# Mixture-of-experts stage: weight layout, the engines of the low parts and of the down loads, and the place of the gathers

## The chip, the core and the metric

The kernel runs on one core of one Trainium2 chip. The metric is device time in microseconds (us) of one execution. Engines are called TensorE (PE in the profile; PEld is its weight load), VectorE (DVE), ScalarE (ACT), GpSimd (POOL) and SyncE (SP, which only issues DMAs here).

## What is computed

The program is one encoder block over 1024 tokens of 1024 channels: a mixer (Hyena and SSD branches, projections, a gate), a layer norm, and a mixture of experts with a second layer norm. The change touches the experts. Cut to what matters, the reference has:

```python
idx, w = route(h2d, router_w, router_bias)      # 8 of 64 experts for each of 1024 tokens
def step(acc, blk):
    tok, wt, e = blk                             # up to 128 tokens of one expert
    xb = h_pad[tok]                              # gather
    hb = jax.nn.silu(xb @ w_gate[e]) * (xb @ w_up[e])   # 1024 -> 256, twice
    yb = (hb @ w_down[e]) * wt[:, None]          # 256 -> 1024
    return acc.at[tok].add(yb), None             # scatter-add
shared = (jax.nn.silu(h2d @ sh_w_gate) * (h2d @ sh_w_up)) @ sh_w_down
h = layer_norm(alpha * h + routed + shared)
```

All values are float32. Each expert has 3 MB of weights: gate and up of 1024 x 256 each, and down of 256 x 1024.

## The kernel before

The mixer and the router run first, and the experts last, in `moe`. Experts are taken by their rank in tokens; a table of capacities gives the 16 busiest 192 slots each, the next 160, 128 and 112. The order alternates a busy expert and a light one, so that a **round** of two experts has three **blocks**: 128 tokens, then 64 or 32 of the same expert, then 128 or 112 of the light one. There are 96 blocks in 32 rounds. The loop over b is written out by hand and sets each engine's order; nothing reorders it.

Float32 products are made of float32r parts: a value is split into a high part (ScalarE rounds it) and a low part (the rest, by a subtraction of two tiles), and a product takes three matmuls (`mm3`, lines 78 to 80), or two where 64 or 32 tokens leave room for both parts of the tokens side by side (`both_mm`, 1893 and 1895).

An expert's weights come in three **parts** p = 3i + q of 128 x 2048 values (1 MB): q = 0 and 1 hold gate and up of four k each, q = 2 holds down. For each part:

- `w_load` issues the load into `eraw` (three tiles for experts of either parity, so six parts are held). Parts 0 and 1 are issued by SyncE, as two DMAs of 512 KB whose pieces in the tile are 256 columns of gate and 256 of up in turn; part 2 by GpSimd, one DMA of 1 MB.
- `w_hi` (line 1643): ScalarE rounds `eraw` into `ehi`.
- `w_lo` (line 1650): `elo = eraw - ehi`, on VectorE for q = 0 and 1, on GpSimd for q = 2.

Step b of the loop handles parts 2b+2 and 2b+3. It issues in this order:

1. `gather(b + 3)`: GpSimd's indirect DMA of the tokens' rows into `xg` (line 1657). Block b's buffer is used again by block b+3.
2. `w_hi` of both parts.
3. The gate and up matmuls of block b, eight k of them. At k = 3 `lo_load(2b+2)`, that is `w_lo` and the load of the part six further, and then `hidden(b - 1)`: TensorE turns the hidden values of the block before, ScalarE and VectorE split them into `hb`.
4. The activation of block b: `swi_act`, or for a small block `both_act` with the tile `lows` (1906 to 1909).
5. `xpose(b + 2)`: eight transposes of the gathered tokens (line 1672), and their split.
6. `lo_load(2b + 3)`, one step of the slot tables of the next group of 12 blocks (one-hot comparisons of line 2103 on VectorE, small matmuls of 2111), if any is left.
7. `down(b - 1)`: the down matmuls of the block before, the copy into `yo` (two tiles), and the scatter-add into `scr_acc` on GpSimd (line 1693). The scatter-adds all write one tensor, and each waits until the one ahead has landed.

DMAs that GpSimd issues are in the profile's queue q0, those of SyncE in q1. On a queue of issues, a wait holds up everything behind it.

Of the kernel before, what the change touches and what calls it, by code (L numbers as in the profile page):

```python
# [9 lines left out]
F32 = mybir.dt.float32  # L10
# [31 lines left out]
class Kern:  # L42
# [1199 lines left out]
    def merge(self):  # L1242
# [106 lines left out]
        with ExitStack() as cx:  # L1349
# [136 lines left out]
                    sh[q] = [[v[:, h * 512:(h + 1) * 512] for v in hl] for h in range(2)]  # L1486

            def sh_gu(t):
                gu = [sh[k // 2][k % 2] for k in range(8)]
                for k, ps in enumerate(self.swi_gu(lhs(t), gu, P)):  # L1490
                    if k < 7:
                        yield
                yield self.swi_act(pool, ps, P, ld()[:, 0:256])
# [100 lines left out]
    def moe(self):  # L1594
# [3 lines left out]
        with ExitStack() as cx:  # L1598
# [17 lines left out]
            def w_load(p):  # L1616
                if p >= 192:
                    return
                i, q = divmod(p, 3)
                eng = nc.gpsimd if q == 2 else nc.sync  # L1620
                if q != 1:
                    weng[0] = eng.value_load(self.eid[0:1, order[i]:order[i] + 1], min_val=0, max_val=63)
                g, u, d = [a[n][0][bass.ds(weng[0], 1)].rearrange("o (p j) c -> (o p) j c", p=P)
                           for n in ("exp_w_gate", "exp_w_up", "exp_w_down")]
                parts = ((g[:, 0:4], u[:, 0:4]), (g[:, 4:8], u[:, 4:8]), (d,))[q]
                wraw[p] = rps[i % 2].tile([P, 2048], F32, name="eraw", bufs=3)
                v = wraw[p].rearrange("p (k c) -> p k c", k=parts[0].shape[1])
                c0 = 0
                for src in parts:
                    n = src.shape[2]  # L1630
                    eng.dma_start(v[:, :, c0:c0 + n], src)
                    c0 += n

            def w_hi(p, c=slice(0, 2048)):
                if p >= 192:
                    return
                if p not in whl:
                    i, q = divmod(p, 3)
                    hi, lo = whl[p] = [wps[i % 2].tile([P, 2048], F32R, name=f"e{c}", bufs=3) for c in ("hi", "lo")]
                    k = 2 if q == 2 else 4  # L1640
                    wsplit.setdefault(i, []).extend(zip(*[[v.rearrange("p (k c) -> p k c", k=k)[:, j] for j in range(k)]
                                                          for v in (hi, lo)]))
                nc.scalar.copy(whl[p][0][:, c], wraw[p][:, c])  # L1643

            def w_lo(p, c=slice(0, 2048)):
                if p >= 192:
                    return
                eng = nc.gpsimd if p % 3 == 2 else nc.vector
                hi, lo = whl[p]
                eng.tensor_tensor(lo[:, c], wraw[p][:, c], hi[:, c].bitcast(F32), ALU.subtract)  # L1650

            def gather(b):
                if b >= len(blocks):
# [28 lines left out]
            def down(b):  # L1682
# [1 line left out]
                    return  # L1684
                i, r, s, o, n = blocks[b]
                y = pool.tile([P, D], F32, name="yo", bufs=2)
                wd = [[(h[:, q * 512:(q + 1) * 512], l[:, q * 512:(q + 1) * 512]) for q in range(2)] for h, l in wsplit[i][8:10]]
                if n in (32, 64):
                    self.both_down(hbs.pop(b), wd, y, n)
                else:  # L1690
# [45 lines left out]
            for p in range(3, 6):  # L1736
                w_load(p)
            xpose(0)
            for p in range(2):
                for c in [slice(c * 512, c * 512 + 512) for c in range(4)]:  # L1740
                    w_hi(p, c)
                    w_lo(p, c)
                w_load(p + 6)
            xpose(1)
            tj = iter(())

            def lo_load(p):
                w_lo(p)
                w_load(p + 6)
            for b, (i, r, s, o, n) in enumerate(blocks):  # L1750
                if s == 0:
                    if i % 8 == 0 and i < 56:
                        for _ in tj:
                            pass
                        tj = table_jobs(i // 8 + 2)
                gather(b + 3)
                w_hi(2 * b + 2)
                w_hi(2 * b + 3)
                x, gu = xts.pop(b), wsplit[i][0:8]
                for k, ps in enumerate((self.both_gu if n in (32, 64) else self.swi_gu)(x, gu, n)):  # L1760
                    if k == 3:
                        lo_load(2 * b + 2)
                        hidden(b - 1)
                if n in (32, 64):
                    sgs[b] = self.both_act(pool, ps, tabs[r][s][2], n)
                else:
                    sgs[b] = self.swi_act(pool, ps, n)
                xpose(b + 2)
                lo_load(2 * b + 3)
                next(tj, None)  # L1770
                down(b - 1)
            for _ in tj:
                pass
# [80 lines left out]

    def swi_gu(self, lhs, gu, n):
        ps = self.bank()
        for k in range(8):
            self.mm3(ps[:n, :], lhs[k][0], lhs[k][1], gu[k][0], gu[k][1], k == 0, k == 7)
            yield ps

    def swi_act(self, pool, ps, n, sg=None):
# [34 lines left out]

    def both_gu(self, x, gu, n):
        ps = self.bank()
        for k in range(8):
            self.both_mm(ps, x[:, k], n, gu[k][0], gu[k][1], k == 0, k == 7)  # L1900
            yield ps

    def both_act(self, pool, ps, w, n):
# [499 lines left out]
```

## Time and profile before

| what | us |
|---|---|
| median of 3 runs (3575.53 to 3591.15) | 3579.17 |
| span of the profiled execution | 3579.6 |
| experts, in that span | about 2440 to 3520 |
| stretch read below as "the stage" | 2480 to 3520 |

The profile is of one execution. Busy time is the time in which an engine has an instruction of its own running; idle time before an instruction is put down to what released it. For TensorE the profile also gives the clock that was granted, as a share of full speed. For the DMA engines it gives packets, bytes, and the time that the packets took as a share of 16 engines.

### The profile page before, as it was taken

The page shows a single profiled execution, that of the slowest core. Times are in us where ns is not written, and L with a number is a line of the kernel's source. Part 1 is how long each engine was busy: PE and PEld are TensorE (multiplying, and loading weights), DVE is VectorE, ACT ScalarE, POOL GpSimd, SP SyncE. Part 2 cuts the span into 40 slices and gives each one's busy share as a digit, 9 for nine tenths or more (in the row PEclk, how much of TensorE's full clock was granted, in tenths as well). Part 3 has the DMA queues.
Part 4 walks back from the last instruction along what each step waited for, and adds up shares of the span by engine and source line. Part 5 has one row for each costly group of instructions (what it writes and reads, how often), then busy time and mean ns, then how long its engine had stood idle before and what let it go on. Part 6 is the DMA issues. An engine that isn't in the chain of part 4 may idle for free. (4 is left out here: it accounts for less than half of the span.)

```text
span 3579.6 us, 43779 instructions
## 1 busy us (share of the span) xinstructions
PE 3186.1 (89%) x15498; PEld 2534.1 (71%) x15499; DVE 2645.1 (74%) x3492; ACT 1462.2 (41%) x2335; POOL 1869.6 (52%) x1610
## 2 busy tenths in 40 slices
PE   8989989998998998998888999988898888898893
PEld 6767777777777776667778888876676666666662
DVE  6788887878787878557997254656787787786775
ACT  3333334343334232323334212324566655555663
POOL 2545454545454656445785140123676676776674
PEclk9999999999999999898889999988999999988996
DMA  4323243223232324734225345326999999988894
GB/s 130 77 71 91 65 90 89 75 76 88 75 84 67 94 77 123 218 124 170 72 71 165 124 165 160 102 72 217 269 264 273 272 262 265 261 246 247 252 283 125
DMA packets 440345, 541.44 MB, mean 151 GB/s; under 512 B 24409, under 2 KB 373373, under 8 KB 431165
## 3 DMA queue, kind: packets, MB, share of 16 engines
q1 hardware_dynamic: 404285, 376.08, 36.0%
q0 software_dynamic: 34688, 158.36, 15.3%
q10 hardware_dynamic: 1152, 4.19, 0.3%
q8 instruction: 123, 2.02, 0.2%
q14 instruction: 97, 0.79, 0.1%
HBM read 433.44 MB, written 105.12 MB: 150 GB/s over the span
## 5 line engine op out<-in xcount | busy, mean ns | idle before, releaser
L170 PE MATMUL bankA<-xth,whi 128*128 128x512 f32 (+1 forms) x1424 | 467.7, 410 | 0.4 <-DVE xtl L74 0.2
L170 PE MATMUL bankA<-xtl,whi 128*128 128x512 f32 (+1 forms) x1424 | 451.4, 399 | 0.0
L170 PE MATMUL bankA<-xth,wlo 128*128 128x512 f32 (+1 forms) x1424 | 447.3, 396 | 1.5 <-POOL wlo L74 1.5
L1650 DVE TENSOR_TENSOR elo<-eraw,ehi 128x2048 fp32r<-128x2048 f32 (+1 forms) x134 | 391.0, 2925 | 15.4 <-ACT ehi L1643 11.3
L1693 POOL DMA_INDIRECT scr_acc<-yo,sidx x96 | 231.3, 2410 | 284.7 <-DMA scr_acc<-yo,sidx 150.9
L74 POOL TENSOR_TENSOR wlo<-wraw,whi 128x1024 fp32r<-128x1024 f32 (+1 forms) x89 | 225.2, 2531 | 279.9 <-ACT whi L73 279.9
L1643 ACT CAST ehi<-eraw 128x2048 fp32r<-128x2048 f32 (+1 forms) x198 | 356.3, 1852 | 3.3 <-DVE sr L1505 3.3
L170 PEld LDWEIGHTS bankA<-xtl,whi 128*128 128x128 f32 (+1 forms) x1424 | 273.2, 192 | 63.7 <-DVE xtl L74 0.3
L170 PEld LDWEIGHTS bankA<-xth,wlo 128*128 128x128 f32 (+1 forms) x1424 | 271.3, 191 | 64.8 <-POOL wlo L74 1.9
L399 POOL TENSOR_SCALAR Wm<-cbm,dt 128x128 f32<-128x128 f32 x256 | 129.8, 507 | 347.2 <-DVE cbm L373 347.2
L170 PEld LDWEIGHTS bankA<-xth,whi 128*128 128x128 f32 (+1 forms) x1424 | 266.0, 194 | 58.0 <-issue 5.6
L1650 POOL TENSOR_TENSOR elo<-eraw,ehi 128x2048 fp32r<-128x2048 f32 x64 | 298.2, 4660 | 13.3 <-ACT ehi L1643 7.5
L78 PE MATMUL bankA<-ehi,xgh 128*128 128x512 f32 (+1 forms) x512 | 210.7, 412 | 0.0
L79 PE MATMUL bankA<-elo,xgh 128*128 128x512 f32 (+1 forms) x512 | 204.5, 399 | 6.0 <-DVE elo L1650 6.0
L80 PE MATMUL bankA<-ehi,xgl 128*128 128x512 f32 (+1 forms) x512 | 203.6, 398 | 0.0
L1657 POOL DMA_INDIRECT xg<-scr_h,gidx x96 | 166.7, 1737 | 63.3 <-issue 24.8
L1672 PE MATMUL bankB<-ident,xg 128*128 128x128 f32 (+3 forms) x768 | 113.8, 295 | 87.0 <-DMA xg<-scr_h,gidx 84.6
L1672 PEld LDWEIGHTS bankB<-ident,xg 128*128 128x128 f32 (+3 forms) x768 | 102.4, 198 | 115.3 <-issue 98.4
L74 DVE TENSOR_TENSOR xgl<-bankB,xgh 128x512 fp32r<-128x512 f32 (+1 forms) x128 | 81.2, 664 | 103.9 <-ACT xgh L73 95.7
L80 PE MATMUL bankA<-ehi,hb 128*128 128x512 f32 (+1 forms) x256 | 119.8, 468 | 28.9 <-DVE hb L74 28.9
L1909 DVE SCALAR_TENSOR_TENSOR lows<-lows,wt 64x256 f32<-64x256 f32 (+1 forms) x32 | 132.1, 4128 | 15.5 <-ACT lows L1908 15.5
L393 DVE SCALAR_TENSOR_TENSOR Em<-bcs,Acs,Em 128x128 f32<-128x128 f32 x256 | 141.1, 610 | 2.3
(586 smaller groups left out, 8410.5 us busy)
## 6 DMA issues: line engine op xcount, KB each, us to landing
eraw<-in_exp_w_gate_dram SPq DMA_DIRECT2D x128, 512.0 KB
eraw<-in_exp_w_down_dram POOLq DMA_DIRECT2D x64, 1024.0 KB, 5.3
eraw<-in_exp_w_up_dram SPq DMA_DIRECT2D x128, 512.0 KB
wraw<-in_w_in_dram SPq DMA_DIRECT2D x88, 512.0 KB
bcs<-scr_at SPq DMA_DIRECT2D x128, 256.0 KB
scr_K<-kout SPq DMA_DIRECT2D x32, 512.0 KB
Kt<-scr_K SPq DMA_DIRECT2D x32, 512.0 KB
scr_gate<-accf SPq DMA_DIRECT2D x16, 512.0 KB
```

Of the source, the lines that this page charges most:

```text
L74: (lo_eng or nc.vector).tensor_tensor(lo, src, hi.bitcast(F32), ALU.subtract)
L78: mm(out, sh, mh, start=first, stop=False)
L79: mm(out, sh, ml, start=False, stop=False)
L80: mm(out, sl, mh, start=False, stop=last)
L170: mm(ps[h], wt[:, k, :n], x[:, h * 512:(h + 1) * 512], start=(k == 0 and f == 1), stop=(k == KT - 1 and l == 1))
L393: STT(E[:, h], bcs[:, 1, h], self.A[:, c, 32 + j:33 + j], E[:, h], ALU.subtract, ALU.min)
L1643: nc.scalar.copy(whl[p][0][:, c], wraw[p][:, c])
L1650: eng.tensor_tensor(lo[:, c], wraw[p][:, c], hi[:, c].bitcast(F32), ALU.subtract)
L1657: nc.gpsimd.indirect_dma_start(out=t[:n, :], out_offset=None, in_=self.h_d, in_offset=bass.IndirectOffsetOnAxis(ap=tabs[r][s][0], axis=0))
L1672: nc.tensor.transpose(ps[:, j * P:j * P + n], free(t[:n, k:k + 1], [[8, P]]), self.ident[:n, :n])
L1693: nc.gpsimd.indirect_dma_start(out=self.acc_d, out_offset=bass.IndirectOffsetOnAxis(ap=tabs[r][s][1], axis=0), in_=y[:n, :], in_offset=Non ...
L1909: nc.vector.scalar_tensor_tensor(t[:, 0:256], t[:, 0:256], w, t[:, 256:512], ALU.mult, ALU.mult)
```

## The change

Five edits, all around the experts:

- **Layout of gate and up.** A part of gate and up lies in `eraw` as 1024 values of gate (four k) and then 1024 of up; each of its two DMAs has one 4 KB piece in every partition. The split tiles are read as two runs of 256 columns, one from each half, and the output bank is given in the same shape. The shared expert's tiles keep their place and are only given in that shape.
- **Low parts.** `w_lo` is on VectorE for all three parts.
- **Down weights.** All loads are issued by SyncE, in the order of the parts.
- **Gathers.** Step b issues `gather(b + 5)` right behind `xpose(b + 2)`, ahead of the scatter of block b-1. Blocks 3 and 4 are gathered before the loop. Since slot tables are needed sooner, the first two experts of a group make two table steps in each of their three steps.
- **Order at k = 3.** `hidden(b - 1)` is ahead of `lo_load(2b + 2)`.

```diff
             def sh_gu(t):
-                gu = [sh[k // 2][k % 2] for k in range(8)]
+                gu = [[v.rearrange("p (s c) -> p s c", s=2) for v in sh[k // 2][k % 2]] for k in range(8)]
...
-                eng = nc.gpsimd if q == 2 else nc.sync
-                if q != 1:
+                eng = nc.sync
+                if q == 0:
                     weng[0] = eng.value_load(self.eid[0:1, order[i]:order[i] + 1], min_val=0, max_val=63)
...
-                v = wraw[p].rearrange("p (k c) -> p k c", k=parts[0].shape[1])
-                c0 = 0
-                for src in parts:
-                    n = src.shape[2]
-                    eng.dma_start(v[:, :, c0:c0 + n], src)
-                    c0 += n
+                v = wraw[p].rearrange("p (s k c) -> p s k c", s=len(parts), k=parts[0].shape[1])
+                for n, src in enumerate(parts):
+                    eng.dma_start(v[:, n], src)
...
-                    k = 2 if q == 2 else 4
-                    wsplit.setdefault(i, []).extend(zip(*[[v.rearrange("p (k c) -> p k c", k=k)[:, j] for j in range(k)]
+                    k, n = (2, 1) if q == 2 else (4, 2)
+                    wsplit.setdefault(i, []).extend(zip(*[[v.rearrange("p (s k c) -> p k s c", s=n, k=k)[:, j] for j in range(k)]
                                                           for v in (hi, lo)]))
...
             def w_lo(p, c=slice(0, 2048)):
                 if p >= 192:
                     return
-                eng = nc.gpsimd if p % 3 == 2 else nc.vector
                 hi, lo = whl[p]
-                eng.tensor_tensor(lo[:, c], wraw[p][:, c], hi[:, c].bitcast(F32), ALU.subtract)
+                nc.vector.tensor_tensor(lo[:, c], wraw[p][:, c], hi[:, c].bitcast(F32), ALU.subtract)
...
             xpose(0)
+            gather(3)
...
             xpose(1)
+            gather(4)
...
-                gather(b + 3)
                 w_hi(2 * b + 2)
                 w_hi(2 * b + 3)
...
                     if k == 3:
+                        hidden(b - 1)
                         lo_load(2 * b + 2)
-                        hidden(b - 1)
...
                 xpose(b + 2)
+                gather(b + 5)
                 lo_load(2 * b + 3)
-                next(tj, None)
+                for _ in range(2 if i % 8 < 2 else 1):
+                    next(tj, None)
                 down(b - 1)
...
     def swi_gu(self, lhs, gu, n):
         ps = self.bank()
+        p3 = ps[:n, :].rearrange("p (s c) -> p s c", s=2)
         for k in range(8):
-            self.mm3(ps[:n, :], lhs[k][0], lhs[k][1], gu[k][0], gu[k][1], k == 0, k == 7)
+            self.mm3(p3, lhs[k][0], lhs[k][1], gu[k][0], gu[k][1], k == 0, k == 7)
...
     def both_gu(self, x, gu, n):
         ps = self.bank()
+        p3 = ps.rearrange("p (s c) -> p s c", s=2)
         for k in range(8):
-            self.both_mm(ps, x[:, k], n, gu[k][0], gu[k][1], k == 0, k == 7)
+            self.both_mm(p3, x[:, k], n, gu[k][0], gu[k][1], k == 0, k == 7)
```

How the instructions stand in the built programs, at three places in the middle of the experts. The first is GpSimd, a round before (`xg` is a gather, `scr_acc` a scatter-add, `elo` a low part, `eid` the expert's number that a load needs):

```order
L1693 DMA scr_acc<-yo,sidx_19823 1152x1024
L1657 DMA xg<-scr_h,gidx_20949 128x1024
L1650 TENSOR_TENSOR elo<-eraw,ehi 128x2048
L1622 TENSOR_LOAD eid
L1622 ISA x2
L1631 ISA
L1631 DMA eraw<-in_exp_w_down_dram 128x2048
L1693 DMA scr_acc<-yo,sidx_19810 1152x1024
L1657 DMA xg<-scr_h,gidx_20962 64x1024
```

and GpSimd now:

```order
L1653 DMA xg<-scr_h,gidx_20616 128x1024
L1689 DMA scr_acc<-yo,sidx_19801 1152x1024
L1653 DMA xg<-scr_h,gidx_20629 64x1024
L1689 DMA scr_acc<-yo,sidx_19814 1152x1024
L1653 DMA xg<-scr_h,gidx_20616 128x1024
```

Nothing is left on GpSimd between a gather and a scatter; what these rows don't tell is that the gather is now for the block six further than that of the scatter behind it, where it was for the one five further than that of the scatter ahead of it.

The second is VectorE over the steps of a small block's followers before (`hb` is the split of the hidden values, `xgl` and `xgh` that of the tokens, `sg` the activation, `yo` the output):

```order
L1650 TENSOR_TENSOR elo<-eraw,ehi 128x2048
L74 TENSOR_TENSOR hb<-bankC,hb 128x2x64
L1866 TENSOR_TENSOR sg<-sg,bankA 128x256
L74 TENSOR_TENSOR xgh<-bankB,xgh 128x4x64 x2
L1650 TENSOR_TENSOR elo<-eraw,ehi 128x2048
L1931 TENSOR_TENSOR yo<-yo,bankA 64x512 x2
L74 TENSOR_TENSOR hb<-bankC,hb 128x256
L1866 TENSOR_TENSOR sg<-sg,bankA 128x256
```

and VectorE now:

```order
L74 TENSOR_TENSOR hb<-bankC,hb 128x2x64
L1646 TENSOR_TENSOR elo<-eraw,ehi 128x2048
L1866 TENSOR_TENSOR sg<-sg,bankA 128x256
L74 TENSOR_TENSOR xgh<-bankB,xgh 128x4x64 x2
L1646 TENSOR_TENSOR elo<-eraw,ehi 128x2048
L1932 TENSOR_TENSOR yo<-yo,bankA 64x512 x2
L74 TENSOR_TENSOR hb<-bankC,hb 128x256
L1646 TENSOR_TENSOR elo<-eraw,ehi 128x2048
L1866 TENSOR_TENSOR sg<-sg,bankA 128x256
```

The subtraction stands behind `hb` and no longer ahead of it, and every step has two of them.

The third is SyncE, the loads of one expert before:

```order
L1622 TENSOR_LOAD eid
L1622 ISA x2
L1631 ISA
L1631 DMA eraw<-in_exp_w_gate_dram 128x4x256
L1631 ISA
L1631 DMA eraw<-in_exp_w_up_dram 128x4x256
```

and SyncE now:

```order
L1629 DMA eraw<-in_exp_w_gate_dram 128x1024
L1629 ISA
L1629 DMA eraw<-in_exp_w_up_dram 128x1024
L1629 ISA
L1629 DMA eraw<-in_exp_w_down_dram 128x2048
L1622 TENSOR_LOAD eid
L1622 ISA x2
```

A gate or up load has rows of 1024 values, and the down load stands behind both parts of gate and up.

## Rows read from the trace of the kernel before

**Rows 1.** Busy us of each engine (instructions), granted clock, DMA share, GB/s, by stretch.
```profile
2480.00:3520.00 1040.00, 919.81 (x4599) 691.16 (x4598) 798.75 (x788) 620.93 (x779) 713.22 (x308) 0.93 0.89 256
2600.00:2700.00 100.00, 89.64 (x463) 70.22 (x463) 79.17 (x78) 59.71 (x74) 70.71 (x31) 0.90 0.93 268
200.00:300.00 100.00, 94.59 (x429) 76.47 (x429) 76.63 (x123) 38.15 (x69) 46.94 (x60) 0.94 0.34 84
2000.00:2100.00 100.00, 100.00 (x437) 81.90 (x437) 39.03 (x40) 22.84 (x34) 37.73 (x40) 1.00 0.41 135
```
**Rows 2.** TensorE's waits from 2480 to 3520: us in total, times, longest.
```profile
PE bankB L1672 <- DMA xg<-scr_h,gidx: 84.6, 30, 5.4
PE bankA L80 <- DVE hb L74: 23.4, 18, 1.8
```
**Rows 3.** Groups from 2480 to 3520: busy us, mean ns, idle us before.
```profile
L1650 DVE TENSOR_TENSOR elo<-eraw,ehi 128x2048 fp32r<-128x2048 f32 x124 | 372.8, 3010 | 11.4 <-ACT ehi L1643 11.3
L1643 ACT CAST ehi<-eraw 128x2048 fp32r<-128x2048 f32 x186 | 344.6, 1904 | 0.0
L1650 POOL TENSOR_TENSOR elo<-eraw,ehi 128x2048 fp32r<-128x2048 f32 x62 | 287.8, 4642 | 1.1
L1909 DVE SCALAR_TENSOR_TENSOR lows<-lows,wt 32x256 f32<-32x256 f32 (+1 forms) x31 | 131.6, 4246 | 15.0 <-ACT lows L1908 15.0
L2103 DVE TENSOR_TENSOR oh<-iota,posm 128x1536 bf16<-128x1536 int16 (+1 forms) x54 | 79.7, 1477 | 0.0
```
**Rows 4.** GpSimd's timeline, 2800 to 2836: start, us, instruction, idle before.
```profile
2803.20 0.58 POOL L1631 DMA_DIRECT2D eraw<-in_exp_w_down_dram  x1 [0.30 <-POOL elo L1650]
2804.08 2.45 POOL L1693 DMA_INDIRECT scr_acc<-yo,sidx  x1 [0.30 <-issue]
...
2814.64 0.59 POOL L1631 DMA_DIRECT2D eraw<-in_exp_w_down_dram  x1 [0.30 <-POOL elo L1650]
2816.38 4.29 POOL L1693 DMA_INDIRECT scr_acc<-yo,sidx  x1 [1.15 <-ACT ehi L1643]
2820.97 1.00 POOL L1657 DMA_INDIRECT xg<-scr_h,gidx  x1 [0.30 <-issue]
2829.95 1.46 POOL L1693 DMA_INDIRECT scr_acc<-yo,sidx  x1 [7.99 <-DVE sg L1866]
```
**Rows 5.** Landing of the scatter issued at 2804.08, from its start.
```profile
DMA to landing us min/median/max: 11.5/11.5/11.5
```
**Rows 6.** Landing of the scatter issued at 2816.38, from its start.
```profile
DMA to landing us min/median/max: 12.8/12.8/12.8
```
**Rows 7.** Landing of the scatter issued at 2829.95, a small block's.
```profile
DMA to landing us min/median/max: 4.8/4.8/4.8
```
**Rows 8.** TensorE's timeline, 2800 to 2836.
```profile
2809.32 0.50 PE L80 MATMUL bankA<-ehi,hb 128*128 128x512 f32 x1 [1.17 <-DVE hb L74]
...
2831.02 1.13 PE L1672 MATMUL bankB<-ident,xg 128*128 128x128 f32 x8 [2.31 <-DMA xg<-scr_h,gidx]
```
**Rows 9.** TensorE's timeline, 2468 to 2480.
```profile
2475.90 0.80 PE L80 MATMUL bankA<-ehi,hb 128*128 128x512 f32 x1 [5.48 <-DVE hb L74]
```
**Rows 10.** VectorE's timeline, 2440 to 2480.
```profile
2468.92 6.60 DVE L1650 TENSOR_TENSOR elo<-eraw,ehi 128x2048 fp32r<-128x2048 f32 x1
...
2476.92 0.48 DVE L1909 SCALAR_TENSOR_TENSOR lows<-lows,wt 64x256 f32<-64x256 f32 x1 [0.48 <-ACT lows L1908]
```
**Rows 11.** VectorE's timeline, 2800 to 2836.
```profile
2816.89 2.27 DVE L1650 TENSOR_TENSOR elo<-eraw,ehi 128x2048 fp32r<-128x2048 f32 x1
```
**Rows 12.** DMA queues from 2480 to 3520: packets, MB, share of 16 engines.
```profile
q0 software_dynamic: 29934, 138.08, 46.1%
q1 hardware_dynamic: 127168, 126.90, 42.3%
```
**Rows 13.** The only data queue from 2817 to 2818 (1 KB pieces).
```profile
q1 hardware_dynamic: 380, 0.38, 108.3%
```
**Rows 14.** The only queue from 2840 to 2842 (8 KB pieces).
```profile
q0 software_dynamic: 96, 0.79, 100.7%
```

More of the change, by code (lines that the diff above doesn't have):

```diff
@@ L1686, in down @@
                 y = pool.tile([P, D], F32, name="yo", bufs=2)
-                wd = [[(h[:, q * 512:(q + 1) * 512], l[:, q * 512:(q + 1) * 512]) for q in range(2)] for h, l in wsplit[i][8:10]]
+                wd = [[(h[:, 0, q * 512:(q + 1) * 512], l[:, 0, q * 512:(q + 1) * 512]) for q in range(2)] for h, l in wsplit[i][8:10]]
                 if n in (32, 64):
```

## The prediction

> **What bounds the kernel now.** I began with the busy time of each engine by stretch, since the change touches the experts alone. In the 1040 us from 2480 to 3520, where the experts run, TensorE is busy 919.81 us, so it is idle for 120.2; VectorE is busy 798.75, GpSimd 713.22, and the 16 DMA engines 89% [rows 1]. No engine is full, so the question is who holds up whom. The waits of TensorE come next: 84.6 of the 120.2 idle us stand before the transposes of the gathered tokens, until a gather has landed, in 30 places; another 23.4 are for `hb`, the low part that VectorE makes of the hidden values [rows 2]. The rows of `lows<-lows` say how many rounds the stretch holds: 31 [rows 3]. A round is an expert of two blocks and an expert of one (three steps of the block loop), and takes 1040/31 = 33.5 us. So one of the three gathers in each round is late.
>
> Why it is late is read from GpSimd's timeline. The scatter-add of 2816.38 is issued 0.8 us after the one of 2804.08 has landed (it takes 11.5 us), the next, 2829.95, 0.8 us after the landing of the second (12.8 us) [rows 4 to 7]. Scatter-adds go into one tensor, each waits for the one ahead, and GpSimd works in order: the gather stands behind it and is issued only at 2820.97. TensorE reaches the transposes that need it and waits 2.31 us, until 2831.02 [rows 4, 8]. The weights are not late: ScalarE, which rounds them first, was idle 0.0 us before its casts [rows 3].
>
> Two more things are to be seen. Where VectorE and GpSimd both subtract, both suffer: the same 128x2048 subtraction takes 2.27 us on VectorE beside a scatter and 6.60 beside GpSimd's own subtraction [rows 10, 11]; the small product into `lows` takes 0.48 us once and 4246 ns in the mean [rows 3, 10]. And TensorE's granted clock is 0.93 in the stage, against 1.00 in a stretch where it is busy for 100 of 100 us and 0.94 where it is busy for 94.59 [rows 1]: with its idle time it loses 0.07 x 1040 = 73 us of full rate (a mean of its two levels, 2.4 GHz at 1.00 and 1.2 GHz).
>
> **The change, part by part.** All sums are against the profiled execution, whose span of 3579.6 us lies within 0.5 us of the median 3579.17.
>
> Gathers ahead. The gather of block b+5 is now issued in step b, ahead of the scatter of block b-1; before, it was the gather of b+3, behind the scatter of b-2. It gains two steps, some 22 us. It adds a wait: its buffer is that of block b+2, freed by transposes that TensorE has just been given. Behind that wait on GpSimd stands only the scatter of b-1, whose matmuls come after the same transposes, so nothing is held up that was free. I take off all 84.6 us. The table work runs ahead too: in three of a group's twelve steps it is issued twice. In such a round VectorE has six one-hot comparisons of 1477 ns, 8.9 us, beside 6 x 2.27 of subtractions and its other work: (798.75 - 372.8 - 131.6 - 79.7)/31 = 6.9 us a round, and 0.5 for `lows` [rows 1, 3, 10, 11]. That is 29.9 us, about the whole of the new round; I add 1.5 us in each of seven groups, +10 (0 to 25).
>
> Low parts on VectorE. GpSimd loses 287.8 us of subtractions, VectorE gains 62. If all 186 run at 2.27 us, they are 422 us in place of 372.8, and `lows` falls from 131.6 to 31 x 0.48 = 15. VectorE ends at 798.75 - 372.8 - 131.6 + 422 + 15 = 731 us: less than before, since the collision goes. At the old mean of 3010 ns it would be 560 + 294 + 132 = 986 of 1040; I take 731, because the slow ones in the rows stand beside GpSimd's subtraction and the quick one beside a scatter [rows 3, 10, 11].
>
> `hidden` ahead of the subtraction. The `hb` wait of 1.17 us at 2809.32 is shorter than the 2.27 us subtraction that stood ahead of it [rows 8, 11]. But the subtraction that GpSimd did is now ahead in the step before. Of 23.4 us [rows 2] I take off 18 (between all of it and +10). Ahead of 2480 one more such wait goes, 5.48 us behind a subtraction of 6.60: -5 [rows 9, 10].
>
> Down weights from SyncE. GpSimd no longer issues them (0.58 us each [rows 4]); SyncE issues them in the order of the parts, behind gate and up of the same expert, when the subtraction of the part six earlier is done; no load waits for a later part than before. They leave the queue that the scatters use. That cannot be priced from one row: the two scatters with a down load just ahead of them land 9.0 and 8.5 us after their issue is written, the one without 3.3, though it moves half the rows [rows 4 to 7]. I count nothing for it; it is what makes room in a rival below.
>
> Long runs. Gate and up now lie as 4 KB pieces. In the stage q1's 126.90 MB take 42.3% of 16 x 1040 us, 55 ns a KB (1000 bytes); in a stretch with nothing but 1 KB pieces it is 45.6 ns, in one with 8 KB pieces 40.8 [rows 12 to 14]. So the gain is 10% to 26% of 440 us of every DMA engine's time: 47 to 117. I take 53, near the low end, since the price of contention stays. On TensorE the moving operand of a gate and up matmul is now two runs of 256 columns; no row shows one. I take nothing; each 10 ns on 64 of them a round would cost 31 x 64 x 10 = 20 us. At the start the first chunk of a part no longer holds gate and up of one k: the first matmuls wait for two more quarter subtractions (0.57 us) in each of two parts, +3.
>
> Clock. With most of the idle time gone I expect some of the 73 us back, and take -25 (0 to -73): the stretch at 94.59% still has 0.94 [rows 1].
>
> **The sum.** TensorE's side of the stage: 1040 - 84.6 - 18 + 10 - 25 = 922 us. The DMA side: 0.89 x 1040 = 926, less 53 is 873 us of work; the highest share that a stretch of 100 us shows is 0.93 [rows 1], and at that it takes 938. The larger ends last: the stage falls by 102, the start gives -5 + 3. 3579.6 - 104 = 3475 us. What is late next is then the weights, held by the DMA engines, with TensorE close behind.
>
> **Rivals.** (a) More comes back: the clock in full and the low price of long runs. TensorE 1040 - 84.6 - 23.4 - 73 = 859, DMA (926 - 117)/0.93 = 870: 170 less, 3410. Against it: both extremes at once.
>
> (b) Long runs give nothing, and the DMA engines are the bound: 926/0.93 = 996, 44 less and 2 for the start, 3533. For it: with 0.93 they are near full already. Against it: the pure stretches differ.
>
> (c) The scatter chain stays as it is. It asks 11.5 + 12.8 + 4.8 + 3 x 0.8 = 31.5 us a round [rows 5 to 7], so 31 x 31.5 = 977: 63 less, 65 with the start, 3514. The gathers no longer wait, but the output buffers (two) do, and TensorE behind them. Then the move of the down loads has not shortened a landing. The Trainium skill (DMA: Bandwidth & Descriptors, "Issuing engines are not separate DMA queues") says that issuing from another engine saves only the issuing sequencer's time; by that, this case is the one to expect. The landings of 9.0 and 3.3 us after issue speak against the rule, though the rows moved differ.
>
> (d) Slower: the scatter chain grows. A scatter is written in 1.46 us when VectorE is at other work and in 4.29 beside a subtraction [rows 4, 11]. VectorE now subtracts for 422 us of some 930. If every scatter took 4.29 and landed as late as now, the chain would be 31.5 + 1.84 + 2.83 = 36.2 us a round, 1121 in all: 81 more, 3659. It decides from 33.5 us a round, so when the three grow by over 2 us together. Against it: the two slow landings should shorten without the down loads ahead. The Trainium skill (SBUF — State Buffer, "Who interferes with whom") holds that a subtraction of two SBUF inputs takes only the read side of the shared port, and that writing descriptors wants the other; by that this case could not be. Here the trace differs: 4.29 us beside one, 1.46 without.
>
> **How the numbers follow.** The forecast, 3475, has 0.58 and by itself runs from 3435 to 3510; (a) 0.12; (b) 0.10; (c) 0.13; (d) 0.05; small changes from other mishaps 0.02. The range of 8 in 10 leaves out (d), the lower half of (a) and the rest: 3425 to 3545. About 0.5%, 18 us, is what a measurement of this kernel can tell from no change. Below 3561 lie the forecast, (a), (b) and (c): faster 0.92; same 0.03; slower 0.05.
>
> **What would show it.** Right: TensorE's wait on gathers near nothing; the VectorE subtraction at a mean of about 2.3 us and `lows` under 0.6; q1 under 50 ns a KB; landings of large scatters well below 11 us; a clock above 0.95. Wrong: waits of ScalarE's casts on the weights (b), of the output copies or GpSimd on the scatter ahead all the time (c, d), or gate and up matmuls longer than 410 ns at full clock.

## The result, and the profile after

The changed kernel takes 3613.65 us (median of 5 runs, 3609.53 to 3617.34); the kernel before took 3579.17 (3568.96 to 3591.15) on the same chip. The ratio is 1.0092, with a 95% interval of 1.0069 to 1.0115: slower by 0.9%, more than the 0.5% that the prediction takes as tellable from no change, 139 us above the forecast and 69 above the upper end of the range. The profiled execution has a span of 3615.6 us.

The expert stage by stretch, for the whole stage and for one round and a half of it; columns as in [rows 1]:

```profile
2480.00:3520.00 1040.00, 884.61 (x4478) 676.30 (x4476) 707.31 (x833) 596.50 (x757) 332.82 (x180) 0.91 0.84 252
2732.00:2780.00 48.00, 32.81 (x171) 26.01 (x171) 30.18 (x30) 22.22 (x29) 13.97 (x8) 0.82 0.84 252
```

TensorE is idle for 155 us of the 1040, against 120 before [rows 1], and its mean clock fell from 0.93 to 0.91. GpSimd is busy for less than half of what it was, VectorE for 91 us less, and the other engines and the DMAs are less busy too, in part since the longer stage puts less of itself into the 1040 us (182 weight subtractions in all, where it was 124 + 62). In the 48 us from 2732 TensorE is busy for only 32.8. So something new is waited for. TensorE's waits from 2480 to 3520 (us in total, times, longest) are now these, in place of [rows 2]:

```profile
PE bankD L2112 <- DVE oh L2104: 128.8, 20, 9.2
PE bankA L78 <- ACT hb L73: 26.5, 9, 4.3
```

The 84.6 us for the gathers are gone, and so are the 23.4 for the low part of `hb`. In their place stand 128.8 us in 20 places, before the small matmuls of the routing tables (L2112), until VectorE has made a one-hot. In the kernel before that wait came to 7.1 us in 8 places, 1.5 at the longest:

```profile
PE bankD L2111 <- DVE oh L2103: 7.1, 8, 1.5
```

The groups of the stage (busy us, mean ns, idle us before), which answer [rows 3]:

```profile
L1646 DVE TENSOR_TENSOR elo<-eraw,ehi 128x2048 fp32r<-128x2048 f32 x182 | 415.1, 2281 | 0.3
...
L2104 DVE TENSOR_TENSOR oh<-iota,posm 128x1536 bf16<-128x1536 int16 (+1 forms) x54 | 78.5, 1484 | 0.0
...
L2112 PE MATMUL bankD<-aux,oh 128*128 128x6 bf16 (+1 forms) x656 | 32.5, 175 | 128.8 <-DVE oh L2104 128.8
...
L1910 DVE SCALAR_TENSOR_TENSOR lows<-lows,wt 64x256 f32<-64x256 f32 (+1 forms) x31 | 14.7, 475 | 15.0 <-ACT lows L1909 15.0
```

The one-hots are as many and as quick as before: 54 of 1.48 us. They are not made late because VectorE is full (707 of 1040 us). They are late because of where they stand.

### One pass of the loop, read from three timelines

The 48 us from 2732 show it. TensorE (start, us, instruction, idle before):

```profile
2755.41 0.90 PE L2112 MATMUL bankD<-aux,oh 128*128 128x6 bf16 x16 [6.03 <-DVE oh L2104]
...
2765.34 0.34 PE L2112 MATMUL bankD<-aux,oh 128*128 128x6 bf16 x8
2774.84 0.89 PE L2112 MATMUL bankD<-aux,oh 128*128 128x6 bf16 x16 [9.16 <-DVE oh L2104]
...
2776.68 0.63 PE L80 MATMUL bankA<-ehi,hb 128*128 128x512 f32 x1
...
2779.95 0.39 PE L79 MATMUL bankA<-elo,hb 128*128 128x512 f32 x1
```

ScalarE:

```profile
2759.25 0.69 ACT L1688 ACTIVATE yo<-bankA,wt 128x512 f32<-128x512 f32 x1 [9.19 <-PE bankA L80]
2760.72 0.69 ACT L1688 ACTIVATE yo<-bankA,wt 128x512 f32<-128x512 f32 x1 [0.78 <-PE bankA L80]
2761.30 3.69 ACT L1640 CAST ehi<-eraw 128x2048 fp32r<-128x2048 f32 x2
2764.90 0.38 ACT L73 ACTIVATE hb<-bankC 128x256 fp32r<-128x256 f32 x1
```

VectorE:

```profile
2765.31 0.42 DVE L74 TENSOR_TENSOR hb<-bankC,hb 128x256 fp32r<-128x256 f32 x1 [8.82 <-ACT hb L73]
2765.65 2.28 DVE L1646 TENSOR_TENSOR elo<-eraw,ehi 128x2048 fp32r<-128x2048 f32 x1
...
2769.62 1.29 DVE L74 TENSOR_TENSOR xgl<-bankB,xgh 128x512 fp32r<-128x512 f32 x2
2770.83 2.28 DVE L1646 TENSOR_TENSOR elo<-eraw,ehi 128x2048 fp32r<-128x2048 f32 x1
2773.03 2.89 DVE L2104 TENSOR_TENSOR oh<-iota,posm 128x1536 bf16<-128x1536 int16 x2
```

Read them in a circle. At 2755.41 TensorE gets its one-hot and does the table matmuls and the down matmuls behind them. At 2759.25 ScalarE, idle for 9.19 us, can copy the first half of their result; behind the copies stand the casts of two weight parts (3.69 us) and behind these the copy into `hb`, 2764.90. VectorE, idle for 8.82 us, takes `hb` and then, in its order, a weight subtraction, the small work of `lows`, `xgl`, a second subtraction and at 2773.03 the two one-hots. The first is ready when TensorE's table matmuls start, 2774.84; the down matmuls stand behind these, and the circle begins again. TensorE's share is 3.8 us (to 2759.25), ScalarE's 6.1 (to 2765.31), VectorE's 9.5 (to 2774.84): 19.4 us for a step of the block loop, where a step took 33.5/3 = 11.2 in the kernel before. Each of the three engines is idle for some 9 us or more of it. (The eight table matmuls of 2765.34 wait for nothing: they are those of the block's first table step, whose one-hot was made in the block before.)

Why the change closes this circle: a table step makes the one-hot of a slot r and issues the matmuls of slot r-1. With one table step to a block of the loop, the one-hot had been made a block earlier. With two in a block, the second step's matmuls need the one-hot that the first step of the same block makes, and that stands last in VectorE's block. Program order had given a lead of one block, and the change took it away in three blocks of every group of twelve. Behind such a wait the next down matmuls run 0.63 us each and then 0.39 again; the granted clock is 0.50 from 2775.60 to 2779.60 (the lower level, 1.2 GHz), after 9.16 idle us, and 0.99 from 2779.70 to 2784. So the lower level of the clock is paid too.

### The profile page after: what moved, and what is told of

The parts are those of the page before. It is cut to its first block, busy times and chain, and to the rows that moved or that the text cites. A ratio compares the mean times of both kernels' runs of the same rounds, so it can differ in the third digit from the quotient of the medians.

```text
span 3615.6 us, 43535 instructions
## 1 busy us (share of the span) xinstructions
PE 3179.0 (88%) x15499; PEld 2540.3 (70%) x15499; DVE 2564.1 (71%) x3556; ACT 1455.5 (40%) x2335; POOL 1487.9 (41%) x1482
## 3 DMA queue, kind: packets, MB, share of 16 engines
q10 hardware_dynamic: 1152, 4.19, 0.3%
## 5 line engine op out<-in xcount | busy, mean ns | idle before, releaser
L1689 POOL DMA_INDIRECT scr_acc<-yo,sidx x96 | 199.2, 2074 | 617.0 <-DMA scr_acc<-yo,sidx 161.2
L1646 DVE TENSOR_TENSOR elo<-eraw,ehi 128x2048 fp32r<-128x2048 f32 (+1 forms) x198 | 438.2, 2216 | 6.9 <-ACT ehi L1640 6.6
L74 DVE TENSOR_TENSOR hb<-bankC,hb 128x256 fp32r<-128x256 f32 (+3 forms) x96 | 34.8, 362 | 295.4 <-ACT hb L73 295.4
L1653 POOL DMA_INDIRECT xg<-scr_h,gidx x96 | 152.9, 1593 | 211.8 <-PE bankB L1668 78.4
L1688 ACT ACTIVATE yo<-bankA,wt 128x512 f32<-128x512 f32 (+1 forms) x128 | 84.5, 691 | 205.2 <-PE bankA L80 151.5
L2112 PE MATMUL bankD<-aux,oh 128*128 128x6 bf16 (+1 forms) x672 | 33.4, 175 | 134.3 <-DVE oh L2104 134.3
L430 DVE TENSOR_TENSOR yt<-yt,off 128x256 f32<-128x256 f32 x112 | 136.0, 1214 | 3.9
L394 ACT ACTIVATE Em<-Em 128x512 f32<-128x512 f32 x64 | 40.4, 631 | 224.8 <-DVE Em L393 224.8
```

Of the source, the lines that this page charges most:

```text
L74: (lo_eng or nc.vector).tensor_tensor(lo, src, hi.bitcast(F32), ALU.subtract)
L430: TT(y, y, off[:, d], ALU.add)
L1646: nc.vector.tensor_tensor(lo[:, c], wraw[p][:, c], hi[:, c].bitcast(F32), ALU.subtract)
L1653: nc.gpsimd.indirect_dma_start(out=t[:n, :], out_offset=None, in_=self.h_d, in_offset=bass.IndirectOffsetOnAxis(ap=tabs[r][s][0], axis=0))
L1689: nc.gpsimd.indirect_dma_start(out=self.acc_d, out_offset=bass.IndirectOffsetOnAxis(ap=tabs[r][s][1], axis=0), in_=y[:n, :], in_offset=Non ...
```

## The experiments

The theory: the lost lead of the table steps costs what the result shows, and without it the rest of the change gains. The rival: the new load and order of VectorE, the queues or the scatters are to blame, and the wait at L2112 only shows what is late anyway. All ratios are to the kernel before on the same chip.

### One table step a block (e1), and the doubled step alone (e2)

e1 is the changed kernel with one table step in each block; the tables of a group are begun two experts earlier so that they are ready in time.

```diff
-                    if i % 8 == 0 and i < 56:
+                    if (i == 0 or i % 8 == 6) and i < 54:
...
-                        tj = table_jobs(i // 8 + 2)
+                        tj = table_jobs((i + 2) // 8 + 2)
...
-                for _ in range(2 if i % 8 < 2 else 1):
+                for _ in range(2 if i < 2 else 1):
                     next(tj, None)
```

> The changed kernel, but with one table step in a block: a group's tables are begun three blocks earlier (at the seventh expert of the group before) in place of two steps in each of three blocks. Only the first group, which has no group before it, keeps the two steps. Theory A (lost lead): in the changed kernel the small table matmuls stand in the very step in which VectorE makes their one-hot, so TensorE waits for VectorE, VectorE for the hidden values, these for ScalarE and ScalarE for TensorE's down matmuls; with the lead of one step back, TensorE's wait of 128.8 us on one-hots goes, every round is about as long as the undisturbed ones (27 us, against 42 and 46 in each group's first two), and some 200 to 240 us go: 3375 to 3415. Theory B (VectorE has too much to do with six comparisons in a round): the same, since the comparisons are spread. Theory C (the loss is from something else, scatters or weights): 3550 or more, and the wait moves elsewhere.

Measured: 3479.62 us, 0.9719 (0.9703 to 0.9736). e2 is the kernel before with the doubled step and nothing else of the change:

```diff
-                next(tj, None)
+                for _ in range(2 if i % 8 < 2 else 1):
+                    next(tj, None)
```

> The kernel before with one edit: two table steps in each of the first three blocks of a group. Theory A: the same loop closes here too, at about 20 places; 6 us each and the clock behind them, less what the late gathers hid: 3640 to 3740. Theory B: VectorE has 25.8 us of work in a round of 33.5, and three comparisons more are 4.4 us, which fit: 3575 to 3600.

Measured: 3693.80 us, 1.0316 (1.0298 to 1.0333). TensorE's waits in e1, 2480 to 3380, and then in e2, 2480 to 3520:

```profile
PE bankA L78 <- ACT hb L73: 48.3, 22, 4.2
PE bankD L2112 <- DVE oh L2104: 4.9, 2, 4.7
```
```profile
PE bankD L2112 <- DVE oh L2104: 137.6, 20, 9.1
PE bankB L1672 <- DMA xg<-scr_h,gidx: 53.4, 25, 4.5
```

The same wait, again in 20 places, appears in the kernel before with that one line, and all but goes from the changed kernel without it (4.9 us in 2 places). The doubled step costs 115 us in the one (within what was expected) and 134 in the other. That settles the sign. e1 gained less than was expected of it (3375 to 3415): with the wait gone, something else held the stage.

### The same two steps, with the lead kept (e3)

e1 also spreads VectorE's one-hots. e3 keeps both table steps in the same blocks, with the same work, and only lets the matmuls follow two steps behind their one-hot and go ahead of the next one.

```diff
-        late = None
-        for r, caps in group + [(None, None)]:
-            if late:
+        wait, lag = [], 1 if ohs else 2
+        for step, (r, caps) in enumerate(group + [(None, None)] * lag):
+            if step:
                 yield
+            if step >= lag:
+                r0, caps0, oh0 = wait.pop(0)
+                ...
             if r is not None:
                 ...
                 TT(oh, ...)
-            if late is not None:
-                r0, caps0, oh0 = late
-                ...
-            late = (r, caps, oh)
+                wait.append((r, caps, oh))
```

> The changed kernel with its two table steps in a block, but the matmuls of an expert's table are issued two table steps behind its one-hot, so always in a later block. VectorE and TensorE have the same work in the same blocks. Theory A: the wait on one-hots goes, 3375 to 3430. Theory B: the overload of VectorE stays, 3590 to 3620.

Measured: 3460.13 us, 0.9661 (0.9644 to 0.9678). Nothing of VectorE's load was taken away, and 154 us went (0.0431 of 3579, by the two ratios). So the cost was the lead and not the load. But 3460 is 30 us above the upper end of what was expected. First the stretch 2480 to 3380 of e3, then the waits of three engines in it, then GpSimd's timeline, then VectorE's subtractions from 2480 to 3300:

```profile
2480.00:3380.00 900.00, 848.34 (x4493) 648.15 (x4492) 709.84 (x839) 596.50 (x763) 320.04 (x181) 0.98 0.96 294
```
```profile
POOL scr_acc L1689 <- DMA scr_acc<-yo,sidx: 134.1, 23, 9.5
ACT yo L1688 <- DMA scr_acc<-yo,sidx: 101.6, 25, 5.9
...
PE bankA L78 <- ACT hb L73: 51.3, 23, 4.1
```
```profile
2803.49 1.58 POOL L1689 DMA_INDIRECT scr_acc<-yo,sidx  x1 [5.53 <-ACT xgh L73]
...
2810.61 1.59 POOL L1689 DMA_INDIRECT scr_acc<-yo,sidx  x1 [3.48 <-ACT yo L1931]
...
2822.87 1.91 POOL L1689 DMA_INDIRECT scr_acc<-yo,sidx  x1 [8.18 <-issue]
...
2831.23 1.59 POOL L1689 DMA_INDIRECT scr_acc<-yo,sidx  x1 [5.16 <-ACT xgh L73]
```
```profile
L1646 DVE TENSOR_TENSOR elo<-eraw,ehi 128x2048 fp32r<-128x2048 f32 x167 | 381.0, 2281 | 0.0
```

The scatter of 2803.49 lands after 6.3 us and that of 2822.87 after 7.6; the next one starts 0.8 us behind each. The scatter between them has no landing on record; the next one starts 12.3 us behind it. The chain of scatters of [rows 4 to 7] is still there and takes 27.7 us for the three in this round. In the mean a round is longer: six weight subtractions make one, and from 2480 to 3300 there are 167, so 29.5 us (33.5 in the kernel before). ScalarE waits for that chain before the output copies (the two output buffers are taken), the copy into `hb` stands behind these on ScalarE, and TensorE waits 51.3 us for that. This is rival (c) of the prediction, with a round of 29.5 us in place of its 31.5.

### The parts of the change on top of e3

**Long runs (e4: e1 with 1 KB pieces).**

```diff
-                v = wraw[p].rearrange("p (s k c) -> p s k c", s=len(parts), k=parts[0].shape[1])
-                for n, src in enumerate(parts):
-                    eng.dma_start(v[:, n], src)
+                v = wraw[p].rearrange("p (k c) -> p k c", k=parts[0].shape[1])
+                c0 = 0
+                for src in parts:
+                    n = src.shape[2]
+                    eng.dma_start(v[:, :, c0:c0 + n], src)
+                    c0 += n
...
-                    wsplit.setdefault(i, []).extend(zip(*[[v.rearrange("p (s k c) -> p k s c", s=n, k=k)[:, j] for j in range(k)]
+                    wsplit.setdefault(i, []).extend(zip(*[[v.rearrange("p (k s c) -> p k s c", s=n, k=k)[:, j] for j in range(k)]
```

> As e1_tables_once, but gate and up lie as before, in 1 KB pieces in turn. If the DMA engines are the bound once the gathers are early (rival b of the prediction): the stage at 926/0.93 = 996 us, so 100 us or more above e1, about 3500. If TensorE is the bound and the pieces only take more of idle DMA time: within 15 us of e1.

Measured: 3475.15 us, 0.9710 (0.9691 to 0.9729), against 0.9719 for e1 on the same chip: no difference. Where the scatters bind, this could not show; e11 below asks again where they do not.

**Late gathers (e5: e3 with the gather of b+3 at the head of the step, as before).**

```diff
-            gather(3)
...
-            gather(4)
...
+                gather(b + 3)
                 w_hi(2 * b + 2)
...
-                gather(b + 5)
```

> e3_lag_two (all parts of the change, table matmuls two steps behind) with the gathers put back: gather of b+3 at the head of step b, behind the scatter of b-2. Theory: TensorE waits for gathers again, as long as before or longer since the rounds are shorter (84.6 us before): 3530 to 3580. Rival: the scatter chain sets the pace now whatever the gathers do: 3455 to 3475.

Measured: 3481.34 us, 0.9720 (0.9693 to 0.9747), between the two expectations. TensorE waits for gathers again, from 2480 to 3380:

```profile
PE bankB L1668 <- DMA xg<-scr_h,gidx: 57.7, 34, 7.1
```

But 57.7 us of wait are worth 0.6%, some 21 us: what the early gathers save at the transposes comes back in good part as TensorE's wait for `hb`, which is 51.3 us in e3 and not among TensorE's waits in e5.

**Low parts of the down weights back on GpSimd (e6: e3 with that alone undone).**

```diff
-                nc.vector.tensor_tensor(lo[:, c], wraw[p][:, c], hi[:, c].bitcast(F32), ALU.subtract)
+                eng = nc.gpsimd if p % 3 == 2 else nc.vector
+                eng.tensor_tensor(lo[:, c], wraw[p][:, c], hi[:, c].bitcast(F32), ALU.subtract)
```

> e3_lag_two with the low parts of the down weights back on GpSimd. Theory A (the collision of the two subtractions is what the move took away): VectorE's subtraction is at 5 us where they meet and the product into lows at 4.2, scatters queue behind 4.6 us of GpSimd's own, the chain grows: 3500 to 3570. Theory B (the move only shifts work between engines with room): 3450 to 3475.

Measured: 3586.65 us, 1.0022 (1.0011 to 1.0034). The whole gain of e3 is gone, 0.036 of 3580 = 129 us; both expectations were too low. The groups of the subtraction and of the product into `lows`, 2480 to 3380, and TensorE's waits there:

```profile
L1647 DVE TENSOR_TENSOR elo<-eraw,ehi 128x2048 fp32r<-128x2048 f32 x108 | 317.4, 2939 | 0.0
...
L1647 POOL TENSOR_TENSOR elo<-eraw,ehi 128x2048 fp32r<-128x2048 f32 x53 | 256.0, 4831 | 0.6
...
L1911 DVE SCALAR_TENSOR_TENSOR lows<-lows,wt 64x256 f32<-64x256 f32 (+1 forms) x27 | 22.3, 827 | 13.0 <-ACT lows L1910 13.0
```
```profile
PE bankA L78 <- ACT hb L73: 64.4, 33, 3.5
PE bankA L79 <- POOL elo L1647: 24.6, 25, 2.2
```

VectorE's subtraction is back at 2.94 us in the mean, from 2.28 in e3, and GpSimd's own of 4.83 us is waited for by TensorE.

**That part alone, on the kernel before (e12).**

```diff
-                eng = nc.gpsimd if p % 3 == 2 else nc.vector
+                eng = nc.vector
```

> The kernel before with one edit: all low parts on VectorE. Theory A: the collision goes, the scatters are issued earlier and with them the gathers: 3500 to 3545. Theory B: 3570 to 3595.

Measured: 3478.12 us, 0.9714 (0.9695 to 0.9732), more than was expected. The group of the subtraction and the stretch 2480 to 3380:

```profile
L1650 DVE TENSOR_TENSOR elo<-eraw,ehi 128x2048 fp32r<-128x2048 f32 x179 | 408.7, 2284 | 51.8 <-ACT ehi L1643 51.7
```
```profile
2480.00:3380.00 900.00, 844.36 (x4412) 641.94 (x4410) 707.42 (x823) 594.94 (x746) 343.96 (x240) 0.96 0.99 290
```

By itself this one line gives 2.9%, where the whole change with the lead kept (e3) gives 3.4%. The DMA engines are at 0.99 here, with the 1 KB pieces.

**Down loads back on GpSimd (e7: e3 with that undone).**

```diff
-                eng = nc.sync
-                if q == 0:
+                eng = nc.gpsimd if q == 2 else nc.sync
+                if q != 1:
```

> e3_lag_two with the down loads issued by GpSimd again, so in the queue of the scatters; the low parts stay on VectorE. In e3 every scatter is issued 0.8 us after the one ahead has landed, 28.7 us a round. Theory A (a down load ahead of a scatter in its queue delays its landing): the two large scatters land 2 us later each, the chain is 33 us a round, 3540 to 3600. Theory B (issuing from another engine only saves the time of the issue): 3450 to 3475.

Measured: 3472.79 us, 0.9702 (0.9681 to 0.9723): 0.4% above e3 by the two ratios, with intervals that all but touch, and within the second expectation. Whether a down load stands ahead of a scatter in its queue matters little for the time. Of the two large scatters of a round one lands as late as in e3 and one later: the medians are 11.1 and 10.0 us here, 10.9 and 8.6 in e3 (2480 to 3380). The time agrees with the rule cited with rival (c) (the Trainium skill, DMA: Bandwidth & Descriptors, "Issuing engines are not separate DMA queues"); the later landing is left open.

### What binds behind the fault: e8, e9, e11, e13

**A third output buffer (e8: e3 with three `yo`, and one `hb` for the space).**

```diff
-                y = pool.tile([P, D], F32, name="yo", bufs=2)
+                y = pool.tile([P, D], F32, name="yo", bufs=3)
...
-            hb = pool.tile([P, 2, 2, P], F32R, name="hb", bufs=2)
+            hb = pool.tile([P, 2, 2, P], F32R, name="hb", bufs=1)
...
```

> e3_lag_two with three output buffers in place of two (and one buffer for the hidden parts in place of two, which frees the room). In e3 ScalarE waits 134 us for scatters that still read an output buffer, and TensorE 52.9 us for the hidden values behind that. If the number of buffers is the limit: 3415 to 3435. If the chain of scatters is, one buffer more only moves the wait: 3450 to 3465.

Measured: 3480.05 us (3463.46 to 3484.74), 0.9723 (0.9700 to 0.9747), above both expectations. TensorE's waits, 2480 to 3380, in the profiled execution of 3463.46:

```profile
PE bankB L1668 <- DMA xg<-scr_h,gidx: 22.0, 12, 3.5
PE bankA L78 <- ACT hb L73: 17.5, 16, 2.2
```

The wait for `hb` shrinks from 51.3 us, and a part of it comes back at the gathers, which stand behind the scatters on GpSimd. A buffer more made no round shorter: 183 weight subtractions in the 900 us, as in e3. The single `hb` may have cost something too; that was not separated.

**Two sums (e9: e3, with the blocks' outputs added into two tensors by turns, so that neighbouring scatters need not wait for each other; the second is cleared in the router's stage and added at the end).**

```diff
-                    out=self.acc_d, out_offset=...
+                    out=(self.acc_d, self.acc2_d)[b % 2], out_offset=...
...
+                nc.sync.dma_start(x2[i], self.acc2_d[i * P:(i + 1) * P, :])
...
+                TT(xs[i][:, c], xs[i][:, c], x2[i][:, c], ALU.add)
...
+            nc.sync.dma_start(self.acc2_d[i // 2 * P:(i // 2 + 1) * P, i % 2 * 512:(i % 2 + 1) * 512], zz)
```

> e3_lag_two with a second sum in memory: blocks of odd number add into it, so a scatter waits for the one two blocks ahead. The second sum is cleared in the router's stage and added at the end (some 10 us of VectorE and 4 MB more to load there, 15 to 20 us). If the chain of scatters bounds e3, the experts fall to the 27 us a round of the undisturbed rounds, 31 x 2 = 60 us less: 3410 to 3430. If TensorE or the DMA engines bound it: 3465 to 3485.

Measured: 3401.59 us (3399.36 to 3407.64), 0.9505 (0.9482 to 0.9527): 5% faster than the kernel before and 6% faster than the changed one, a little below the lower end of what was expected if the chain bounds e3. **The same with 1 KB pieces (e11)**, by the edit of e4:

```diff
-                for n, src in enumerate(parts):
-                    eng.dma_start(v[:, n], src)
...
+                for src in parts:
+                    n = src.shape[2]
+                    eng.dma_start(v[:, :, c0:c0 + n], src)
+                    c0 += n
...
```

> e9_two_sums with gate and up in 1 KB pieces as before. With the chain gone the DMA engines are at 0.96 of their time. If the long runs pay where the DMA engines are the limit: 3415 to 3440. If they pay nothing here either: 3393 to 3410.

Measured: 3401.24 us, 0.9495 (0.9480 to 0.9511). The stretch 2480 to 3300 of e9 and the queue of its weights (packets, MB, share of 16 engines), then the same of e11:

```profile
2480.00:3300.00 820.00, 815.95 (x4404) 624.31 (x4403) 696.86 (x824) 589.29 (x749) 409.10 (x179) 1.00 1.00 319
```
```profile
q1 hardware_dynamic: 43287, 188.30, 65.2%
```
```profile
2480.00:3300.00 820.00, 820.00 (x4429) 628.39 (x4428) 702.41 (x830) 595.04 (x754) 424.99 (x179) 1.00 1.05 320
```
```profile
q1 hardware_dynamic: 135566, 188.97, 69.5%
```

Now TensorE is busy for 816 and 820 of 820 us at full clock, and its waits in the trace come to some 4 us in e9 and none in e11: by these rows TensorE bounds the stage at last. The DMA engines' share is as high, 1.00 and 1.05, but that e11 asks more of them in the same time speaks against them as the bound. Long runs take some 6% off the packets' time (65.2% against 69.5% for the same bytes) and nothing that can be told off the kernel's.

**Two sums on the kernel before (e13), by the edits of e9:**

```diff
-                    out=self.acc_d, out_offset=...
+                    out=(self.acc_d, self.acc2_d)[b % 2], out_offset=...
...
```

> The kernel before with a second sum in memory for the odd blocks (as in e9), nothing else. If the chain of scatters is what made the gathers late in the kernel before: the waits of 84.6 us go, less 15 to 20 for the second sum at the end: 3490 to 3530. If the gathers are late for another reason, GpSimd's subtractions above all: 3580 to 3600.

Measured: 3558.41 us, 0.9936 (0.9919 to 0.9952), between the expectations. TensorE's wait for gathers, 2480 to 3380, stays:

```profile
PE bankB L1673 <- DMA xg<-scr_h,gidx: 83.8, 28, 4.2
```

So in the kernel before the scatter chain was not the only reason for the late gathers. With the chain eased, GpSimd's own subtractions of 4.6 us still stand between them; but they are not the whole of the rest, since in e12, where they are gone, TensorE still waits for gathers and GpSimd, by the profile, waits for ScalarE's casts before it can issue a down load (2480 to 3380 of e12):

```profile
PE bankB L1672 <- DMA xg<-scr_h,gidx: 54.3, 29, 3.7
POOL eraw L1631 <- ACT ehi L1643: 152.0, 28, 5.5
```

e13 also bears on why e12 is faster. Its groups from 2480 to 3380:

```profile
L1651 DVE TENSOR_TENSOR elo<-eraw,ehi 128x2048 fp32r<-128x2048 f32 x112 | 261.7, 2337 | 57.2 <-ACT ehi L1644 57.2
L1651 POOL TENSOR_TENSOR elo<-eraw,ehi 128x2048 fp32r<-128x2048 f32 x56 | 257.2, 4593 | 1.0
...
L1914 DVE SCALAR_TENSOR_TENSOR lows<-lows,wt 64x256 f32<-64x256 f32 (+1 forms) x27 | 113.1, 4191 | 13.1 <-ACT lows L1913 13.1
```

VectorE's subtraction is quick here, 2.34 us in the mean, though GpSimd still does a third of them, and the kernel gains 0.6%. In e6 the product into `lows` is down to 0.83 us, and the time is that of the kernel before. So neither of the two quick operations brings e12's 2.9% by itself.

## Why the prediction was wrong, point by point

- **The step that failed** is the term of the doubled table steps. The prediction priced it as load (six one-hots in a round, 29.9 us of VectorE's work in a round) and put +10 (0 to 25) on TensorE's side. The one-hots did stay at 1.48 us and VectorE below full; but the term was 115 (e2), 134 (e1) and 154 us (e3), because it was one of order. 128.8 of that stand in the rows as waits; the lower clock behind them (0.91 against 0.98 in e3) is probably the rest, less what e3 itself waits for the scatters, though no run parts the two. With 154 in the place of 10, TensorE's side of the prediction's sum is 1066 us, above the DMA side's 938 and the 1040 of before. The order of before could have told it: the one-hot comes last in VectorE's block, behind the weight subtractions, and the matmuls now want it in that block. None of the rivals holds this mechanism. (d) had the sign, by a chain of scatters that did not grow: a scatter is written in 2.07 us in the mean of the changed kernel's stage (2.49 in the kernel before, 2480 to 3380), and the median landing is 8.7 us (10.5 before).
- **Low parts on VectorE: right**, and the heart of the change. Predicted were 2.27 us, 0.48 us and 731 us of VectorE's time; measured 2.28, 0.475 and 707 (for 182 subtractions; the prediction's are 186). But the prediction let it count only through room on VectorE. e12 gives 2.9% for it alone, and e6 loses everything without it.
- **Gathers: the wait went as predicted (84.6 to 0), its worth did not.** It was taken off in full; early gathers are worth some 21 us in e5 against e3, since the scatter chain then holds ScalarE and TensorE.
- **`hidden` ahead of the subtraction:** the 23.4 us for `hb` from VectorE are gone, but 26.5 stand before the copy of `hb` on ScalarE (51.3 in e3). Its order by itself was not tried.
- **Down loads from SyncE:** counted as nothing; 0.4% by e7.
- **Long runs: mis-sized, and the ceiling wrong.** -53 us of DMA time was taken, and 0.93 as the highest share that the DMA engines reach. The packets' time fell by some 6% (e9 against e11: 4.3% of 820 us, 35 us), and e9 and e12 hold shares of 1.00 and 0.99. The "DMA side" of 938 us, which ended the sum, is no bound here: rival (b) rested on the same ceiling and falls with it.
- **Clock: the direction was right** where the waits go: 0.98 in e3, and 1.00 in e9 from 2480 to 3300. In the changed kernel new waits took it to 0.91.
- **The sum without the table fault** would have stayed at 3475, since its DMA side set it, and e3 measures 3460. That is in part luck: the bound that set the sum (DMA) does not exist, and the one that does, the scatter chain, was rival (c) with 31.5 us a round where e3 shows 29.5 in the mean. What stays open is how the gain of e12 splits between VectorE's quicker work and GpSimd's free time. e13 says that the quicker subtractions alone do not bring it; no run parts the rest.

## What to carry to other kernels

In a hand-written order, count the lead between a producer and its consumer in program steps, apart from the load: a thing that is consumed in the step that makes it can tie the in-order engines between into one circle, as it did three here, and the totals of busy time don't show it. Before a wait is booked as a gain, look for the chain that would end next, and try the cheapest break of it; here two sums in place of one were worth 1.6% once the fault was out and 0.6% before. A small part of a change can hide the worth of the rest, so an undo of each part is worth more than a run of the whole.

## What the runs showed of the hardware

The subtraction of 128x2048 takes VectorE 2.28 us in the mean where GpSimd subtracts nothing (the changed kernel, e3, e12). Where GpSimd does a third of them (4.6 to 4.8 us each), the overlap in time decides: from 2480 to 3380 of the kernel before, the 80 of VectorE's that overlap none of GpSimd's take 2.28 us in the mean, the 27 that overlap one 5.18. So the mean over all is 3.01 there, 2.94 in e6, and 2.34 in e13, where 7 of 112 overlap. The product into `lows` takes 0.475 us in the changed kernel, 4.25 and 4.19 in the kernel before [rows 3] and in e13, where all of them overlap a subtraction of GpSimd, and 0.83 in the mean of e6, where 2 of 27 do.

A scatter's issue on GpSimd takes 1.44 us in the mean of the 29 that overlap no subtraction of VectorE, and 3.35 in the mean of the 43 that overlap one by over 0.5 us (2480 to 3380 of the kernel before).

The 16 DMA engines held shares of 0.99 to 1.05 over 800 us and more (a share can pass 1, as in [rows 13]), where the kernel before had shown 0.93 at most in the stretches of 100 us that were read. The kernel's time was the same there with pieces of 1 KB as with pieces of 4 KB (e11, e9).
